# A fixed order on TensorE for the attention part of a decoder trunk: scores in runs of 14 or 16, transposes from the third projection step on, value products of two units in a row

## The chip, the cores and the metric

The kernel runs on one core of a Trainium2 chip. The metric is the device time of one execution in microseconds (us); it is given as the median of several executions. The profile is of one execution, whose own time is given beside it.

## The reference, cut to what matters

One gated short-convolution layer is followed by one layer of dilated sliding-window attention, each with a feed-forward block behind it. There are 512 tokens, 1024 features, 16 heads of 64 and three branches, whose softmaxes are joined by their log-sum-exp. The part that matters here is the attention:

```python
s = jnp.einsum("brhnqd,brhnkd->brhnqk", qb, kk).astype(jnp.float32)
...
s = jnp.where(mask, s, NEG_INF)
m = jnp.max(s, axis=-1)
p = jnp.exp(s - m[..., None])
l = jnp.sum(p, axis=-1)
o = jnp.einsum("brhnqk,brhnkd->brhnqd", p, vv.astype(jnp.float32)) / l[..., None]
lse = m + jnp.log(l)
...
wts = jax.nn.softmax(jnp.stack(lses, axis=0), axis=0)
o = jnp.einsum("gbsh,gbshd->bshd", wts, jnp.stack(outs, axis=0))
return o.astype(x.dtype).reshape(B, S, N_HEADS * HEAD_DIM) @ w_o
```

## The kernel before, in words

All projections split their operands into a high and a low part and run three products. A weight block of 128x8x256 comes in by one DMA as `raw`; VectorE multiplies it by a gain (L113), ScalarE casts the high part `wh` (L93) and VectorE subtracts it to get `wl` (L94). There are buffers for three such blocks (six `wh`, six `wl`) and two for `raw`.

The attention goes over four groups of four heads (`for i in range(NG)`, L757). A group has six projection steps (`rope_mms`, q and k of three branches): each is 48 matmuls of 512 columns into two banks of the tag "mm" (`feature_mm`, L140), and then `rope` (L527): eight ScalarE copies into `sw`, then six VectorE operations. Behind the steps come three value projections (`values`, L645), each in two pieces of 48 matmuls of 256 columns (L658).

Between these the small matmuls of the attention are placed:

- Scores (`scores`, L577): q and k of one head are 64 rows high, and the two heads of a pair stand on rows 0 to 63 and 64 to 127; an output is 128x128 in a bank of the tag "at". VectorE adds the mask, writes `p` and takes the maximum in one operation (L597), ScalarE takes the exponent (L607). There are two parts, two head pairs and four blocks of queries, so 60 score matmuls in a group. The profile shows each as two passes.
- `factors` (L610) exchanges the row sums of the two parts by small DMAs and makes the joint softmax factors.
- `transposed` (L676): VectorE scales `p` by the factor (L685), TensorE transposes it (L688, 60 in a group) into two "at" banks for a unit, ScalarE copies each bank to a tile `trs` (L690). These tiles come from the same four buffers as `sw`.
- `times_v` (L693): value products with 64 output rows (L717, 60 in a group, two passes each) into a bank `o`, which ScalarE copies out.

A unit is one head pair, one part and two of the four blocks, so there are eight in a group. `fill` (L753) runs two entries of a list behind each piece and each step: scores behind the pieces of the value projections, units behind the steps of the next group. Each tag, "mm" and "at", has four PSUM banks. In the last group the first steps of the output projection (`wo_step`, L513) stand where the next group's steps would be, and `heads_x` (L745) writes its operands `xh`, `xl` into the memory that the value projections read.

The code is recorded, and a scheduler then orders the instructions of each engine, unless `tc.issue_after` ties one behind another. It also picks the buffer that a new tile takes. So before the change, where a score matmul or a value product stands among the projections is the scheduler's choice, save for this:

```python
with tc.issue_after(mark) if mark else nullcontext():
    m = nc.tensor.matmul(
        out, v, rhs, start=first, stop=part == 0 and e == 1,
        skip_group_check=True).ins
if first:
    mark = m
```

Of the kernel before, what the change touches and what calls it, by code (L numbers as in the profile page):

```python
# [15 lines left out]
P = 128  # L16
T = 512
NT = T // P
D = 1024
KT = D // P  # L20
# [6 lines left out]
NG = 4  # L27
# [11 lines left out]
def trunk(  # L39
# [82 lines left out]
    def feature_mm(jobs, t0, t1, attn):  # L122
# [15 lines left out]
        for i, (k, p) in enumerate(todo):  # L138
            for ps, (_, (wh, wl)) in zip(outs, jobs):
                nc.tensor.matmul(ps, (wh, wl, wh)[p][:, k, :], x[p == 2][:, k],  # L140
                                 start=i == 0, stop=i == len(todo) - 1)
# [9 lines left out]
    def feature_mms(makers, between=None, attn=False, marks=((),) * 4):  # L151
# [5 lines left out]
        if between is None:  # L157
            pairs = [m() for m in makers]
            for i in range(0, len(pairs), 2):
                feature_mm(pairs[i:i + 2], 0, NT, attn)  # L160
            return [ps for ps, _ in pairs]
# [18 lines left out]
    def token_mm(outs, ah, al, wh, wl, first, last):  # L180

        for i, o in enumerate(outs):
            nc.tensor.matmul(o, ah, wh[i], start=first, stop=False)  # L183
# [329 lines left out]
    def wo_step(k, tt, n):  # L513
        wh, wl = ws[4 * n + k // 2]
        return token_mm([ys[tt][n]], xh[:, tt, k, :], xl[:, tt, k, :],
                        [wh[:, k % 2, :]], [wl[:, k % 2, :]], k == 0, k == KT - 1)

    with ExitStack() as inner:
# [24 lines left out]
        def rope_mms(g, i, rest, fill):  # L543
# [4 lines left out]
            for src, gain in ((w_q[0], gq), (w_kv, gkv)):  # L548
                tag = "at" if ms and rest else "mm"
                ms += makers(tag, load_cols(src, c0), gain)  # L550
                if not rest:
                    d += [rope(ps, f"qk{g}", g) for ps in feature_mms(ms[-2:], None, True)]
# [9 lines left out]
        class Heads:  # L562
# [14 lines left out]
            def scores(self, part, pr, b2):  # L577

                st = self.st[part]
                ps = [bank("at", "s").rearrange("p (b k) -> p b k", b=2) for _ in range(2)]  # L580
                for b in (b2, b2 + 1):
                    for e in range(2):
# [4 lines left out]
                        for h2 in range(2):  # L587
                            rw = slice(64 * h2, 64 * h2 + 64)
                            nc.tensor.matmul(  # L589
                                ps[h2][:, b - b2, e * P:(e + 1) * P],  # L590
                                q[pr][rw, b * P:(b + 1) * P], k[pr][rw, kb * P:(kb + 1) * P],
                                start=True, stop=True)
                    lo = 128 if part == 0 and b == 0 else 0
                    mask = (maskA, maskB)[part]
                    for h2 in range(2):
                        hh = 2 * pr + h2
                        nc.vector.tensor_tensor_reduce(  # L597
                            self.p(part, hh, b), ps[h2][:, b - b2, lo:], mask[:, lo:],
                            1.0, -3.0e38, ALU.add, ALU.max, st[:, b, hh, 0:1])
                if b2 == 0:  # L600
                    return
# [43 lines left out]
            def values(self, g):  # L645
# [7 lines left out]
                def piece(n):  # L653
                    for k in range(KT):
                        wh, wl = (x[:, k % 4, :] for x in w[k // 4])
                        for p in range(3):
                            for m in range(2):
                                nc.tensor.matmul(  # L658
                                    ps[m][:, n, :], (zh, zh, zl)[p][:, k, 2 * m + n],
                                    (wh, wl, wh)[p],  # L660
                                    start=k == 0 and p == 0, stop=k == KT - 1 and p == 2)
# [14 lines left out]
            def transposed(self, pr, part, hh, b2):  # L676
# [5 lines left out]
                for b in (b2, b2 + 1):  # L682
# [4 lines left out]
                    for e in range(lo, 256, P):  # L687
                        nc.tensor.transpose(  # L688
                            tr[:, b - b2, e:e + P], p[:, e - lo:e - lo + P], ident)
# [3 lines left out]
            def times_v(self, pr, part, b2, trs):  # L693
# [5 lines left out]
                mark = None  # L699
                for b in (b2, b2 + 1):  # L700
                    for e in range(2):
                        if part == 0 and b + e == 0:
                            continue
                        for hh in range(2):
# [11 lines left out]
                            with tc.issue_after(mark) if mark else nullcontext():  # L716
                                m = nc.tensor.matmul(  # L717
                                    out, v, rhs, start=first, stop=part == 0 and e == 1,
                                    skip_group_check=True).ins
                            if first:  # L720
                                mark = m
# [8 lines left out]
            def units(self):  # L730

                def unit(pr, part, b2):
                    self.flight.append(((pr, part, b2), [
                        self.transposed(pr, part, hh, b2) for hh in (2 * pr, 2 * pr + 1)]))
                    if len(self.flight) > 1:
                        self.rest()

                return [lambda a=(pr, part, b2): unit(*a)
# [125 lines left out]
```

## Time and profile before

| what | before |
|---|---|
| median of 3 runs | 1498.02 us |
| lowest and highest | 1497.49 and 1499.73 us |
| the profiled execution: its time | 1498.81 us |
| its span | 1497.0 us |
| granted TensorE clock, mean | 0.999 |
| PE busy | 1484.5 us (99%) |
| PEld, DVE, ACT busy | 1256.2, 741.6, 615.6 us |

The span is the time from the first to the last instruction of the program; the execution's time lies 1.8 us above it. PE is TensorE's matmuls, PEld its weight loads, DVE VectorE, ACT ScalarE. Matmuls overlap, so that an instruction's own duration is longer than the time until the next one can start.

### The profile page before, as it was taken

Reading aid. Unit: us, or ns where it says so; the run is one execution under the profiler, and the core shown is the slowest. Engines: PE = TensorE matmul, PEld = TensorE weight load, DVE = VectorE, ACT = ScalarE, POOL = GpSimd, SP = SyncE. Lnnn points to the kernel's source line nnn. Section 1 sums busy time; section 2 is a strip of 40 time slices with the busy share of each in tenths; the row PEclk is TensorE's granted clock in tenths of the full one; section 3 lists DMA queues with packets and bytes.
Section 4 is the critical chain, followed back from the end, with each engine's and each line's share of the span. In section 5 each row is a group of like instructions: output and inputs, shape, how many; then the busy total and the mean of one; then the engine's idle time right before and its main releaser. Section 6 shows DMA issues by size and latency. Waiting matters only on the chain.

```text
span 1497.0 us, 19969 instructions
## 1 busy us (share of the span) xinstructions
PE 1484.5 (99%) x8155; PEld 1256.2 (84%) x8155; DVE 741.6 (50%) x1312; ACT 615.6 (41%) x1133; POOL 58.2 (4%) x108
## 2 busy tenths in 40 slices
PE   9999999999999999999999999999999999999998
PEld 8888898888888889898788889889879888888886
DVE  5735453323233368767667566765546332323332
ACT  5313342212123236574666557466554221212321
POOL 1000100000000020000001001000010000000000
PEclk9999999999999999999999999999999999999999
DMA  6343033223323303222122212212123322332311
GB/s 219 107 141 109 33 113 113 72 98 113 123 88 113 113 29 113 85 86 86 57 65 79 85 64 81 85 57 86 31 85 113 113 71 98 113 124 87 113 57 56
DMA packets 110369, 137.43 MB, mean 92 GB/s; under 512 B 3485, under 2 KB 99013, under 8 KB 110278
## 3 DMA queue, kind: packets, MB, share of 16 engines
q1 hardware_dynamic: 108708, 135.56, 27.2%
q8 instruction: 64, 1.05, 0.3%
q0 software_dynamic: 1280, 0.26, 0.2%
q10 hardware_dynamic: 290, 0.33, 0.1%
q14 instruction: 27, 0.22, 0.0%
HBM read 133.92 MB, written 2.23 MB: 91 GB/s over the span
## 4 chain that ended last, share of the span: by engine, by line
PE 66%; issue 26%; DMA 3%; DVE 2%; POOL 1%; ACT 1%; POOLq 0%; DVEq 0%; SPq 0%; ACTq 0%
PE mmf L140 26%; PE atf L140 14%; PE vps L658 8%; PE s L589 2%; PE o L717 2%; PE tr L688 2%; DMA raw<-in_w_kv 1%; DVE raw L113 1%; DMA raw<-in_ffn_w_gate_up 1%; POOL y L207 1%; DMA raw<-in_w_q 1%; DVE wl L94 1%; POOL a L205 1%; PE y1b L187 0%; PE y1a L183 0%
## 5 line engine op out<-in xcount | busy, mean ns | idle before, releaser
L94 DVE TENSOR_TENSOR wl<-raw,wh 128x1024 fp32r<-128x1024 f32 x244 | 292.9, 1222 | 74.6 <-ACT wh L93 74.2
L93 ACT CAST wh<-raw 128x1024 fp32r<-128x1024 f32 x244 | 246.8, 1047 | 104.3 <-PE atf L140 42.7
L140 PE MATMUL mmf<-xh,wh 128*128 128x512 f32 (+1 forms) x848 | 275.2, 377 | 2.8 <-ACT xh L93 2.8
L140 PE MATMUL mmf<-xl,wh 128*128 128x512 f32 (+1 forms) x848 | 271.4, 374 | 0.0
L140 PE MATMUL mmf<-xh,wl 128*128 128x512 f32 (+1 forms) x848 | 270.7, 374 | 0.0
L140 PE MATMUL atf<-xh,wh 128*128 128x512 f32 (+1 forms) x560 | 181.0, 365 | 0.0
L140 PE MATMUL atf<-xl,wh 128*128 128x512 f32 (+1 forms) x560 | 180.1, 365 | 0.0
L140 PE MATMUL atf<-xh,wl 128*128 128x512 f32 (+1 forms) x560 | 180.0, 365 | 0.0
L140 PEld LDWEIGHTS mmf<-xh,wh 128*128 128x128 f32 x848 | 152.8, 188 | 32.5 <-ACT xh L93 3.5
L366 DVE TENSOR_TENSOR act<-atf,s 128x512 f32<-128x512 f32 x44 | 30.4, 692 | 301.6 <-ACT s L365 301.6
L140 PEld LDWEIGHTS mmf<-xl,wh 128*128 128x128 f32 x848 | 153.3, 188 | 28.7 <-issue 0.9
L140 PEld LDWEIGHTS mmf<-xh,wl 128*128 128x128 f32 x848 | 153.3, 188 | 27.9
L365 ACT ACTIVATE s<-mmf 128x512 f32<-128x512 f32 x44 | 26.3, 598 | 334.9 <-PE mmf L140 326.7
L113 DVE TENSOR_TENSOR raw<-raw,cols 128x512 f32<-128x512 f32 x144 | 90.4, 686 | 85.7 <-DMA raw<-in_w_kv 60.5
L140 PEld LDWEIGHTS atf<-xl,wh 128*128 128x128 f32 x560 | 99.5, 189 | 16.9
L140 PEld LDWEIGHTS atf<-xh,wl 128*128 128x128 f32 x560 | 99.5, 189 | 17.0
L140 PEld LDWEIGHTS atf<-xh,wh 128*128 128x128 f32 x560 | 99.6, 188 | 16.6
L536 ACT COPY sw<-mmf 32x512 f32<-32x512 f32 x92 | 53.3, 579 | 78.7 <-PE mmf L140 71.4
L658 PE MATMUL vps<-wh,xh 128*128 128x256 f32 x384 | 81.2, 289 | 0.0
L658 PE MATMUL vps<-wh,xl 128*128 128x256 f32 x384 | 79.3, 286 | 0.0
L658 PE MATMUL vps<-wl,xh 128*128 128x256 f32 x384 | 79.1, 285 | 0.0
L94 DVE TENSOR_TENSOR al<-act,ah 128x512 fp32r<-128x512 f32 x44 | 30.2, 691 | 96.4 <-ACT ah L93 96.4
(182 smaller groups left out, 1993.6 us busy)
## 6 DMA issues: line engine op xcount, KB each, us to landing
raw<-in_ffn_w_gate_up SPq DMA_DIRECT2D x44, 1024.0 KB, 6.6
raw<-in_w_kv SPq DMA_DIRECT2D x24, 1024.0 KB, 5.2
raw<-in_ffn_w_down SPq DMA_DIRECT2D x22, 1024.0 KB, 4.8
raw<-in_w_q SPq DMA_DIRECT2D x12, 1024.0 KB, 5.2
raw<-in_conv_w_in SPq DMA_DIRECT2D x11, 1024.0 KB, 5.1
raw<-in_conv_w_out SPq DMA_DIRECT2D x4, 1024.0 KB, 4.8
raw<-in_w_o SPq DMA_DIRECT2D x4, 1024.0 KB, 5.0
h<-in_x SPq DMA_DIRECT2D x4, 512.0 KB, 7.1
```

What stands on the lines that cost most here:

```text
L93: return [nc.scalar.copy(hi, src).ins, nc.vector.tensor_tensor(lo, src, hi.bitcast(F32), ALU.subtract).ins]
L94: nc.vector.tensor_tensor(lo, src, hi.bitcast(F32), ALU.subtract).ins]
L113: nc.vector.tensor_tensor(src[:, ks], src[:, ks], g.broadcast_to([P, a // 2, b]), ALU.mult)
L140: nc.tensor.matmul(ps, (wh, wl, wh)[p][:, k, :], x[p == 2][:, k], start=i == 0, stop=i == len(todo) - 1)
L205: nc.gpsimd.tensor_scalar(a, ssq[:, 0:1], EPS, ssq[:, 1:2], ALU.add, ALU.add)
L365: nc.scalar.activation(s, ps[2 * j], AF.Silu)
L366: nc.vector.tensor_tensor(act[2 * c + j], ps[2 * j + 1], s, ALU.mult)
L536: nc.scalar.copy(w[s:s + 32], y[s + 32:s + 64])
L589: nc.tensor.matmul(ps[h2][:, b - b2, e * P:(e + 1) * P], q[pr][rw, b * P:(b + 1) * P], k[pr][rw, kb * P:(kb + 1) * P], start=True, stop=True)
L658: nc.tensor.matmul(ps[m][:, n, :], (zh, zh, zl)[p][:, k, 2 * m + n], (wh, wl, wh)[p], start=k == 0 and p == 0, stop=k == KT - 1 and p == 2)
L688: nc.tensor.transpose(tr[:, b - b2, e:e + P], p[:, e - lo:e - lo + P], ident)
L717: m = nc.tensor.matmul(out, v, rhs, start=first, stop=part == 0 and e == 1, skip_group_check=True).ins
```

## The change

A helper `strict` ties each matmul that goes through it behind the one before it, so that these keep the order of the code. The projection steps (when they get a `fill`), the value projections, scores, transposes, value products and the first output steps all go through it. A call of `scores` now does all four blocks of a head pair: 14 or 16 score matmuls into four "at" banks, then the eight mask operations. `fill` runs one entry, in the middle of a step and behind it, and ahead of each value piece. Three empty entries put the first unit behind the second step. A unit is transposed alone, and every second call first runs the value products of the two units before it.

```diff
+    traced = []
+    def strict(op, *args, **kwargs):
+        with tc.issue_after(traced[0]) if traced else nullcontext():
+            traced[:] = [op(*args, **kwargs).ins]
...
         for i, (k, p) in enumerate(todo):
+            if fill and i == len(todo) // 2:
+                fill()
             for ps, (_, (wh, wl)) in zip(outs, jobs):
...
+                if fill:
+                    strict(nc.tensor.matmul, *args, **kwargs)
...
-            def scores(self, part, pr, b2):
+            def scores(self, part, pr):
 
                 st = self.st[part]
-                ps = [bank("at", "s").rearrange("p (b k) -> p b k", b=2) for _ in range(2)]
-                for b in (b2, b2 + 1):
+                banks = [[bank("at", "s").rearrange("p (b k) -> p b k", b=2) for _ in range(2)]
+                         for _ in range(2)]
+                for b in range(NT):
...
                         for h2 in range(2):
                             rw = slice(64 * h2, 64 * h2 + 64)
-                            nc.tensor.matmul(
-                                ps[h2][:, b - b2, e * P:(e + 1) * P],
-                                q[pr][rw, b * P:(b + 1) * P], k[pr][rw, kb * P:(kb + 1) * P],
-                                start=True, stop=True)
+                            strict(nc.tensor.matmul,
+                                   banks[b // 2][h2][:, b % 2, e * P:(e + 1) * P],
+                                   q[pr][rw, b * P:(b + 1) * P], k[pr][rw, kb * P:(kb + 1) * P],
+                                   start=True, stop=True)
+                for b in range(NT):
                     lo = 128 if part == 0 and b == 0 else 0
...
-                def unit(pr, part, b2):
-                    self.flight.append(((pr, part, b2), [
-                        self.transposed(pr, part, hh, b2) for hh in (2 * pr, 2 * pr + 1)]))
-                    if len(self.flight) > 1:
+                def unit(n, what):
+                    if n % 2 == 0:
                         self.rest()
...
+                    if what:
+                        pr, part, b2 = what
+                        self.flight.append((what, [
+                            self.transposed(pr, part, hh, b2) for hh in (2 * pr, 2 * pr + 1)]))
...
             def rest(self):
-                what, trs = self.flight.pop(0)
-                self.times_v(*what, trs)
+                for what, trs in self.flight:
+                    self.times_v(*what, trs)
+                self.flight.clear()
...
         def fill():
-            for f in todo[:2]:
-                f()
-            del todo[:2]
+            if todo:
+                todo.pop(0)()
...
                 for piece in heads.values(g):
+                    fill()
                     piece()
-                    fill()
             heads.factors()
-            todo = heads.units()
+
+            todo += [lambda: None] * (3 if i < NG - 1 else 0) + heads.units()
```

What the change moves is shown at three places; a row is a line of the code, an operation, output and inputs, and the output's size, and behind "waits" the engines or DMA queues whose semaphores it waits for.

TensorE in the value projections of the second group, before: the score matmuls (`s`) of the second head pair stand singly and by fours among the projection's matmuls (`vps`).

```order
L589 MATMUL s<-qk_5361,qk_5234 128x128
L658 MATMUL vps<-wh,xh 128x256 x2
L658 MATMUL vps<-wl,xh 128x256 x2
L658 MATMUL vps<-wh,xl 128x256 x2
L658 MATMUL vps<-wh,xh 128x256 x2
L658 MATMUL vps<-wl,xh 128x256
L589 MATMUL s<-qk_5361,qk_5234 128x128
L658 MATMUL vps<-wl,xh 128x256
L658 MATMUL vps<-wh,xl 128x256 x2
L658 MATMUL vps<-wh,xh 128x256
L589 MATMUL s<-qk_5361,qk_5234 128x128 x4
```

TensorE at the start of the same value projections, in the changed kernel: the last value products (`o`) of the first group, then all 14 score matmuls of the first head pair, then the first projection's matmuls (all of them come through the helper, L127).

```order
L127 MATMUL o<-trs,v_4618 64x4x32 [waits Activation_49] x2
L127 MATMUL o<-trs,v_4618 64x4x32 x6
L127 MATMUL s<-qk_5307,qk_5225 128x128 [waits PE_49] x2
L127 MATMUL s<-qk_5307,qk_5225 128x128 x4
L127 MATMUL s<-qk_5307,qk_5225 128x128 [waits PE_49]
L127 MATMUL s<-qk_5307,qk_5225 128x128 [waits DVE_49,PE_49]
L127 MATMUL s<-qk_5307,qk_5225 128x128 x6
L127 MATMUL vps<-wh,xh 128x256 x2
```

Value products and scores now follow each other in one piece, 14 instructions each, and the eighth score matmul, the first into the fourth bank, waits for VectorE.

VectorE at that place, in the changed kernel: the gains of a coming block, the low part of the third value projection's weights, and then the first mask operations of these scores (`p,st<-s`).

```order
L113 TENSOR_TENSOR raw<-raw,cols 128x4x128 x3
L94 TENSOR_TENSOR wl<-raw,wh 128x1024 [waits Activation_49] x2
L619 ISA p_5857,st_5859<-s,cst 128x128 [waits DMASW3_49,DMASW2_49,PE_49]
L619 ISA st_5859 128x1
L619 ISA p_5857,st_5859<-s,cst 128x256
```

The mask operations that free the first bank stand behind two weight splits; the program's semaphores say that the eighth score matmul waits for the second mask operation, since its tile takes the bank of the unit's first tile.

VectorE in the last group, in the changed kernel: the end of `factors`, three low parts of the output projection's operand (`xl`), and the scalings of `p` that the transposes wait for.

```order
L661 RECIPROCAL f_8921<-f_8921 128x16 [waits DVE_49]
L94 TENSOR_TENSOR xl<-O,xh 128x4x128 [waits PE_49,Activation_49]
L662 TENSOR_TENSOR f_8907<-f_8907,ea 128x16 [waits DVE_49]
L662 TENSOR_TENSOR f_8921<-f_8921,ea 128x16 [waits DVE_49]
L94 TENSOR_TENSOR xl<-O,xh 128x4x128 [waits PE_49,Activation_49]
L705 TENSOR_SCALAR p_8371<-p_8371,f_8907 128x128 [waits DVE_49]
L94 TENSOR_TENSOR xl<-O,xh 128x4x128 [waits PE_49,Activation_49]
L705 TENSOR_SCALAR p_8372<-p_8372,f_8921 128x256 [waits DVE_49]
```

Before, all six of these low parts stood ahead of `factors`; now three stand between its last operations and the first scaling that a transpose needs, and each waits for the last matmuls of the value projection.

## Rows read from the trace of the kernel before

**Rows 1.** The page: TensorE's busy time, share of the span, instructions.

```profile
PE 1484.5 (99%) x8155; PEld 1256.2 (84%) x8155; DVE 741.6 (50%) x1312; ACT 615.6 (41%) x1133; POOL 58.2 (4%) x108
```

**Rows 2.** Four stretches, by group: length, busy us (instructions) by engine, clock, DMA.

```profile
624.89:756.49 131.60, 131.38 (x877) 111.72 (x876) 89.65 (x213) 80.21 (x173) 6.12 (x10) 1.00 0.25 78
756.49:885.88 129.39, 129.39 (x878) 110.93 (x877) 87.01 (x210) 79.54 (x172) 5.88 (x10) 1.00 0.24 76
885.88:1015.34 129.46, 129.46 (x878) 110.96 (x877) 87.06 (x210) 79.56 (x172) 5.87 (x10) 1.00 0.24 74
1015.34:1099.15 83.81, 83.14 (x673) 72.91 (x671) 40.02 (x140) 50.44 (x127) 5.87 (x10) 1.00 0.14 48
```

**Rows 3.** Timeline of PE, third group: start us, us, engine, line, operation.

```profile
884.06 0.61 PE L140 MATMUL mmf<-xl,wh 128*128 128x512 f32 x2
...
885.88 0.40 PE L658 MATMUL vps<-wh,xh 128*128 128x256 f32 x2
...
891.39 0.40 PE L658 MATMUL vps<-wh,xl 128*128 128x256 f32 x2
891.72 0.94 PE L589 MATMUL s<-qk,qk 64*128 64x128 f32 x12
892.59 0.50 PE L658 MATMUL vps<-wh,xh 128*128 128x256 f32 x2
892.93 0.39 PE L658 MATMUL vps<-wl,xh 128*128 128x256 f32 x2
```

**Rows 4.** Timeline of PE, a score run of 16 passes in the last group.

```profile
1040.07 0.40 PE L658 MATMUL vps<-wh,xl 128*128 128x256 f32 x2
1040.40 1.16 PE L589 MATMUL s<-qk,qk 64*128 64x128 f32 x16
...
1041.83 0.40 PE L658 MATMUL vps<-wl,xh 128*128 128x256 f32 x2
```

**Rows 5.** Timeline of PE, a run of value products between transposes.

```profile
707.04 0.87 PE L688 MATMUL tr<-ident,p 128*128 128x128 f32 x6
707.84 1.09 PE L717 MATMUL o<-trs,v 128*64 128x128 f32 x16
708.87 0.66 PE L688 MATMUL tr<-ident,p 128*128 128x128 f32 x4
709.28 0.48 PE L140 MATMUL mmf<-xh,wh 128*128 128x512 f32 x1
```

**Rows 6.** Timeline of ACT at the end of a group's steps.

```profile
885.90 0.58 ACT L536 COPY sw<-mmf 32x512 f32<-32x512 f32 x1 [5.38 <-PE mmf L140]
...
890.65 1.99 ACT L93 CAST wh<-raw 128x1024 fp32r<-128x1024 f32 x2
```

**Rows 7.** Timeline of DVE behind a run of scores.

```profile
1044.58 0.42 DVE L597 CUSTOM_DVE_ANT_0 p<-s,cst 128x256 f32<-128x256 f32 x1 [1.91 <-PE s L589]
...
1044.93 0.42 DVE L597 CUSTOM_DVE_ANT_0 p<-s,cst 128x256 f32<-128x256 f32 x1
```

**Rows 8.** Timeline of all engines, last group, from its last projections to its transposes.

```profile
1060.24 6.28 DVE L94 TENSOR_TENSOR xl<-O,xh 128x512 fp32r<-128x512 f32 x6 [5.00 <-ACT xh L93]
...
1062.82 0.40 PE L183 MATMUL y<-wh,xh 128*128 128x512 f32 x1
...
1068.21 8.22 DVE L685 TENSOR_SCALAR p<-p,f 128x128 f32<-128x128 f32 x32
...
1074.41 1.91 PE L688 MATMUL tr<-ident,p 128*128 128x128 f32 x16
1075.04 2.06 ACT L690 COPY trs<-tr 128x512 f32<-128x512 f32 x4 [7.66 <-PE tr L688]
```

**Rows 9.** Timeline of all engines, the end of the last group.

```profile
1096.59 1.89 PE L717 MATMUL o<-trs,v 128*64 128x128 f32 x28
...
1099.15 0.50 PE L183 MATMUL y<-wh,xh 128*128 128x512 f32 x1 [0.68 <-ACT xh L93]
...
1100.08 3.50 DVE L94 TENSOR_TENSOR wl<-raw,wh 128x1024 fp32r<-128x1024 f32 x3 [0.26 <-ACT wh L93]
```

More of the change, by code (lines that the diff above doesn't have):

```diff
@@ L178, in makers, with token_mm @@
                 for j in range(2)]
-    def token_mm(outs, ah, al, wh, wl, first, last):
+    def token_mm(outs, ah, al, wh, wl, first, last, strictly=False):
+        if strictly:
+            for i, o in enumerate(outs):
+                strict(nc.tensor.matmul, o, ah, wh[i], start=first, stop=False)
+                strict(nc.tensor.matmul, o, ah, wl[i], start=False, stop=False)
+                strict(nc.tensor.matmul, o, al, wh[i], start=False, stop=last)
+            return
         for i, o in enumerate(outs):
@@ L551, in rope_mms @@
                 if not rest:
-                    d += [rope(ps, f"qk{g}", g) for ps in feature_mms(ms[-2:], None, True)]
+                    d += [rope(ps, f"qk{g}", g) for ps in feature_mms(
+                        ms[-2:], None, True, fill=fill)]
                     fill()
@@ L597, in scores @@
                         nc.vector.tensor_tensor_reduce(
-                            self.p(part, hh, b), ps[h2][:, b - b2, lo:], mask[:, lo:],
+                            self.p(part, hh, b), banks[b // 2][h2][:, b % 2, lo:], mask[:, lo:],
                             1.0, -3.0e38, ALU.add, ALU.max, st[:, b, hh, 0:1])
-                if b2 == 0:
-                    return
                 for hh in (2 * pr, 2 * pr + 1):
@@ L657, in piece @@
                             for m in range(2):
[L658 to L661, printed above, removed]
+                                strict(nc.tensor.matmul,
+                                       ps[m][:, n, :], (zh, zh, zl)[p][:, k, 2 * m + n],
+                                       (wh, wl, wh)[p],
+                                       start=k == 0 and p == 0, stop=k == KT - 1 and p == 2)
                     if n:
@@ L715, in times_v @@
                             first = new and b == 0 and e == 0
[L716 to L721, printed above, removed]
+                            strict(nc.tensor.matmul, out, v, rhs, start=first,
+                                   stop=part == 0 and e == 1, skip_group_check=True)
                 if part == 1 or b2 == 0:
@@ L760, in trunk @@
                   for g in range(NB)]
[L761 to L762 removed]
+            while todo:
+                fill()
             if pp is None:
@@ L766, in trunk @@
             heads = Heads(i, qk)
-            todo = [lambda a=(part, pr, b2): heads.scores(*a)
-                    for part in range(2) for pr in range(2) for b2 in (0, 2)]
+            todo += [lambda a=(part, pr): heads.scores(*a)
+                     for part in range(2) for pr in range(2)]
             for g in range(NB):
                 for piece in heads.values(g):
+                    fill()
                     piece()
-                    fill()
             heads.factors()
-            todo = heads.units()
+            todo += [lambda: None] * (3 if i < NG - 1 else 0) + heads.units()
         load_wo(0)
```

33 lines of the change are left out of this document (16 added, 17 removed).

## The prediction

> **What bounds the kernel now.** I read the busy times first: TensorE (PE) works for 99% of the span, and no other engine reaches 51% [rows 1]. Then the four groups of the attention, each from the end of one group's projection steps to the end of the next group's, the last to its last value product [rows 2]: PE is busy for 131.38 of 131.60 us, 129.39 of 129.39, 129.46 of 129.46, and 83.14 of 83.81, with the clock at 1.00. So there is no wait here that the change could take away. It can only make PE's own work shorter, or add waits. The next question is what PE's time is made of, and for that I read the distances between starts, since matmuls overlap. From 884.06 eight matmuls of 512 columns start in 1.82 us until the projection of values begins at 885.88: 0.2275 each. From there 46 of 256 columns take 5.51 us to 891.39: 0.12 each [rows 3]. A group has 288 of either kind, 65.5 and 34.5 us, and 60 transposes of 0.11, 6.5 us. What is left of a group, scores and value products, is 131.6 − 106.5 = 25.1 us in the first, 22.9 and 23.0 in the next two. The last has 84 matmuls of 512 columns (19.1 us), so 83.8 − 19.1 − 34.5 − 6.5 = 23.7, of which 0.7 are a wait at its end that has nothing to do with the change [rows 9], so 23.0. I forecast **faster**, since this remainder is more than the same products cost in longer runs.
>
> **What a run of scores costs.** A run is a row of small matmuls with nothing else between them. In one of 12 passes, from 891.39 to 892.93 are 1.54 us with four matmuls of 0.12, which leaves 1.06 for the run [rows 3]. In one of 16, from 1040.07 to 1041.83 are 1.76, which leaves 1.28 [rows 4]. The difference of four passes is 0.22, or 0.055 a pass, and 1.06 − 12×0.055 = 0.40 is the price of entering and leaving a run, paid whatever its length. For value products the only row between transposes has 16 passes: from 707.04 to 708.87 are 1.83 us less six transposes, 1.18, so 0.30 and 16×0.055 [rows 5]. That they too cost 0.055 a pass is my choice. The upper bound is the 28 passes of 1.89 us against 16 of 1.09 [rows 5, 9], 0.067 a pass, with a smaller fixed price then.
>
> **What the change removes.** A group has 60 score matmuls and 60 value products, 120 passes each. At 0.055 they are 13.2 us, so about 9.8 of the 23 are prices of entering and leaving; runs of 12 [rows 3] are among the longer ones, others have one or four matmuls, as the order shows. The changed kernel has four runs of scores in a group (28, 28, 32, 32 passes) and four of value products (32, 28, 32, 28). By the prices above these are 2×1.94 + 2×2.16 + 2×2.06 + 2×1.84 = 16.0 us. The saving is 9.1 + 6.9 + 7.0 + 7.0 = 30.0 over the four groups. In the last group the scheduler still parts one run of value products in three, between matmuls of the output projection: two more runs, −0.8. That makes 29.2. At 0.067 a pass for value products (0.10 fixed), their two longer forms cost 2.24 and 1.98, together 0.6 more in a group: 26.6 instead of 29.2.
>
> **What the change adds: the wait for the fourth bank.** In groups 2 to 4 the first run of scores follows at once upon the last run of value products. Its eighth matmul waits until VectorE has read the first tile. From the end of the steps VectorE has two low parts ahead of that, which wait for ScalarE's two casts of 1.0 each [rows 6]. With 0.2 for the first to start, the first low part can begin at about 1.3. The two take 1.17 each [rows 9], to 3.6, and the two mask operations begin 0.35 apart and last 0.42 [rows 7], to 4.35. PE arrives after the value products (1.84) and seven score matmuls (14 passes and half a fixed price, 0.97): 2.8. It then waits 1.5 us, three times: 4.5. Behind this matmul stand seven more and all of the value projection, so nothing covers it. If VectorE placed the masks ahead of the low parts, it would be nothing; the order says that it doesn't.
>
> **What the change adds: the last group.** The first transposes wait for `p` scaled, and VectorE has three low parts `xl` ahead. Six of them take 6.28 now [rows 8], so 1.03 apart. They wait for the value projection's last matmul, since they overwrite what it reads. So a transpose can start about 0.3 + 3×1.03 + 0.2 + 2×0.26 (32 scalings in 8.22 [rows 8]) = 4.2 us behind that matmul; PE has only nine matmuls of the output projection first, 2.05 us. A wait of about 2.2 us, 2.3 with the pipeline. Before, PE did not meet it: its first transpose in these rows comes at 1074.41, 6.2 us after the scalings begin at 1068.21 [rows 8]. Both waits together cost 6.8.
>
> **What I cost at nothing.** The eight mask operations behind a run take 8×0.35 = 2.8 us and hold all four "at" banks [rows 7]; the 48 value-projection matmuls behind each run take 5.76 and cover them [rows 3]. Without that cover each of 16 runs would wait 0.7. Masks and casts themselves do not change in number. The transposes move to where two runs of 24 matmuls of 512 columns (10.9 us) and eight transposes lie between a unit's transposes and its value products, 11.8 in all. ScalarE has two casts (2.0) and eight rope copies (885.90 to 890.65, 4.75 [rows 6]) at a step's end, 6.7 us, and then a unit's two copies, 4 for 2.06 [rows 8], so they are done near 7.8. That leaves 4 us. No DMA is issued at another place in its queue that PE waits for: the traffic in the groups is 0.14 to 0.25 of the engines [rows 2].
>
> The Trainium skill, TensorEngine Tiling (Array Packing), section PSUM Bottleneck, speaks against the change: tiles of the array speed up TensorE but not the emptying of PSUM, and the copies may become the bottleneck. By that rule a run of scores in four banks would be paced by its 2.8 us of mask operations. The cover above, 5.76 us, says no, and the sum goes by the cover; the third rival below prices the other way.
>
> **The sum.** 29.2 − 6.8 = 22.4. The profiled execution took 1498.8, so 1476.4; the median is 0.8 lower, and the same saving from it gives 1475.6. I forecast **1476**. With the other price a pass it is 1478.6. A measurement of this kernel tells about 0.2%, 3 us, from no change.
>
> **The rivals.**
> *No new waits.* VectorE's and ScalarE's queues may run ahead of PE so far that the low parts are done before PE arrives. For it: PE has not once waited in three of the groups. Against it: the casts and the `xl` both need the end of PE's own work just before. It gives 1498 − 29.2 = 1469.
> *Reading the scores paces them.* If the low parts and gains that stand among the masks delay these beyond the cover, each of 16 runs waits about the 0.7 above (2.8 − 2.06), 11.9 us in all. For it: VectorE is busy for 87 of 129 us in a group. Against it: 5.76 of cover. It gives 1476 + 11.9, about 1488.
> *Slower: value products wait for their copies.* The copies to `trs` stand behind casts and rope copies on ScalarE and share four buffers with the latter. If they came 4 us later than worked out, PE would begin to wait at each of the 16 runs, and from 1.4 us of wait a run (22.4/16) the change loses. At 2 us it gives 1498 − 22.4 + 32 = 1508. For it: ScalarE has nine casts or copies ahead of the first of them. Against it: it is idle for 50 of 129 us in a group.
> *The change doesn't do what it says.* If the fixed price were not one of a run but of each pass or of the first product in a bank, longer runs would save nothing, and the waits remain: 1498 + 6.8 = 1505. Against it: 12 and 16 passes differ by 0.055 a pass, far below 1.06/12.
>
> **How the numbers follow.** The forecast has 0.62, with a range of its own of 1472 (half of the waits) to 1481 (the higher price a pass, 2.6, and 2 us of waits more). No new waits has 0.12, pacing by the masks 0.13, the slower rival 0.06, a price that isn't saved 0.03, and 0.04 is left for savings and waits that cancel. The range goes from 1467, a little below the second case, to 1488, and leaves out about 0.15. Faster than 1495 are the first three and no other: 0.87; within 3 us 0.04, slower 0.09.
>
> **What would show it.** Runs of 28 and 32 passes in 1.9 to 2.2 us; groups 2 and 3 (from one end of the steps to the next) of 106.5 + 16.0 + 1.5 = 124.0 us where 129.4 stand; an idle time of PE of 1.5 us ahead of the eighth score matmul in three groups, released by VectorE; one of 2.2 ahead of the last group's first transpose, released by a scaling of `p`; ScalarE's copies of `trs` done 4 us ahead of their products; the clock still at 1.00. The forecast is wrong if a longer run costs over 0.067 a pass, if PE idles over 5 us elsewhere in the groups, or if time is lost outside them, which the change doesn't touch.

## The result

The changed kernel takes 1482.28 us (median of 4, 1480.96 to 1483.45), the kernel before 1498.01 (1497.49 to 1499.73). The ratio is 0.9892, 95% interval 0.9879 to 0.9904: 15.7 us faster. The forecast was 1476; the time lies in its wide range (1467 to 1488), and just above the likeliest case's own range of 1472 to 1481. The profiled execution took 1480.96 with a span of 1479.1, so in the trace the saving is 17.9 where 22.4 were forecast. The points below go by the trace.

### The profile after

By the page (as [rows 1]) TensorE is busy for 1461.5 us, still 99%, of a span that is 17.9 shorter.

The four stretches of the attention, cut as in [rows 2] (at the end of each group's steps and value products):

```profile
624.73:749.23 124.50, 123.54 (x878) 108.53 (x877) 91.54 (x218) 81.25 (x174) 6.13 (x10) 1.00 0.27 86
749.23:873.40 124.17, 122.98 (x879) 108.43 (x877) 86.90 (x211) 79.10 (x173) 5.88 (x10) 1.00 0.24 78
873.40:998.33 124.93, 123.56 (x879) 108.80 (x877) 84.40 (x207) 78.92 (x173) 5.87 (x10) 1.00 0.24 77
998.33:1080.04 81.71, 78.38 (x675) 69.99 (x673) 38.41 (x140) 49.08 (x127) 5.87 (x10) 1.00 0.17 53
```

Against 131.60, 129.39, 129.46 and 83.81 they are 7.1, 5.2, 4.5 and 2.1 us shorter, 18.9 in all. PE is no longer busy for the whole of a stretch: 1.0, 1.2, 1.4 and 3.3 us of each are idle. The view of waits names what ended the idle time (total, times, longest):

```profile
PE s L127 <- DVE st L619: 3.6, 3, 1.2
PE mmf L154 <- ACT xh L93: 2.2, 3, 1.3
...
PE y L127 <- ACT v L686: 1.2, 1, 1.2
PE o L127 <- ACT trs L710: 1.1, 2, 1.0
...
PE tr L127 <- DVE p L705: 0.2, 1, 0.2
```

**The runs.** In PE's timeline a run of 28 score passes stands between two value projections; one starts 1.77 us before the next matmul:

```profile
632.11 0.40 PE L127 MATMUL vps<-wh,xl 128*128 128x256 f32 x2
632.44 1.83 PE L127 MATMUL s<-qk,qk 64*128 64x128 f32 x28
634.21 0.50 PE L127 MATMUL vps<-wh,xh 128*128 128x256 f32 x2
634.55 0.39 PE L127 MATMUL vps<-wl,xh 128*128 128x256 f32 x2
```

From 632.11 to 634.55 are 2.44, less four matmuls of 0.12: 1.96, where 1.94 was worked out. A run of 32 passes, read in the same way at 640.14, costs 2.17 where 2.16 was worked out.

**The wait for the fourth bank.** The first run of the second group, in PE's timeline, right behind the value products, and VectorE's at the same time:

```profile
747.55 1.75 PE L127 MATMUL o<-trs,v 128*64 128x128 f32 x28
749.23 1.16 PE L127 MATMUL s<-qk,qk 64*128 64x128 f32 x14
751.57 1.13 PE L127 MATMUL s<-qk,qk 64*128 64x128 f32 x14 [1.19 <-DVE st L619]
752.62 0.50 PE L127 MATMUL vps<-wh,xh 128*128 128x256 f32 x2
```
```profile
748.51 2.36 DVE L94 TENSOR_TENSOR wl<-raw,wh 128x1024 fp32r<-128x1024 f32 x2 [4.42 <-ACT wh L93]
750.78 0.28 DVE L619 CUSTOM_DVE_ANT_0 p<-s,cst 128x128 f32<-128x128 f32 x1
750.99 0.42 DVE L619 CUSTOM_DVE_ANT_0 p<-s,cst 128x256 f32<-128x256 f32 x1
```

Seven matmuls (14 passes), then the stop; the second mask operation ends at 751.41, and the eighth matmul starts at 751.57, 4.0 behind the steps' end (4.35 was worked out). The run takes 3.39 instead of 1.77: 1.62 lost, three times.

**The copies that I had given 4 us of slack.** ScalarE's and VectorE's timelines ahead of the first group's first value products, which start at 702.19 and stall in the middle; behind them, from all three engines, the lines at the second run of products, which starts at 717.11:

```profile
695.95 1.57 ACT L710 COPY trs<-tr 128x512 f32<-128x512 f32 x3
702.81 0.59 ACT L710 COPY trs<-tr 128x512 f32<-128x512 f32 x1 [5.28 <-DVE qk L559]
```
```profile
698.46 2.50 DVE L113 TENSOR_TENSOR raw<-raw,cols 128x512 f32<-128x512 f32 x4 [0.91 <-DMA raw<-in_w_kv]
700.88 1.22 DVE L94 TENSOR_TENSOR wl<-raw,wh 128x1024 fp32r<-128x1024 f32 x1
702.01 0.69 DVE L559 TENSOR_TENSOR qk<-qk,sw 128x512 f32<-128x512 f32 x1
```
```profile
717.72 0.69 DVE L559 TENSOR_TENSOR qk<-qk,sw 128x512 f32<-128x512 f32 x1
718.51 0.58 ACT L710 COPY trs<-tr 128x512 f32<-128x512 f32 x1 [2.42 <-DVE qk L559]
719.15 1.09 PE L127 MATMUL o<-trs,v 128*64 128x128 f32 x14 [0.96 <-ACT trs L710]
```

Three copies are early, near 697. The fourth needs one of the four buffers, which the rope's last operation frees; that stands on VectorE behind four gains (2.50 us, begun 0.91 late for a weight block's DMA) and a low part (1.22). In the second run of products the stop is longer: there two sets of gains stand ahead of the rope's last operation, and the first waits 3.16 for its DMA. From the start of a run to the next matmul the two runs take 2.27 and 3.06 us; the same two in the second group's products, where the same copies come just in time, take 1.90 and 1.68.

**The last group.** The view books the idle time in another place than forecast: the seventh matmul of the output projection waits for a bank that ScalarE copies out behind three casts of `xh`, and the transposes then hardly wait.

```profile
1044.81 1.07 ACT L686 COPY v<-vps 128x512 f32<-128x512 f32 x2
...
1045.25 1.07 DVE L94 TENSOR_TENSOR xl<-O,xh 128x512 fp32r<-128x512 f32 x1
1045.44 0.50 PE L127 MATMUL y<-wh,xh 128*128 128x512 f32 x1 [1.24 <-ACT v L686]
...
1046.23 2.90 DVE L705 TENSOR_SCALAR p<-p,f 128x256 f32<-128x256 f32 x11
1046.63 1.22 PE L127 MATMUL tr<-ident,p 128*128 128x128 f32 x8 [0.23 <-DVE p L705]
```

The bank hides the forecast wait and does not replace it. The scaling that releases the first transpose stands behind the third `xl`, as forecast, and starts at 1046.23, so the transpose starts at 1046.63, 3.98 behind the value projection's end (1042.65), where 4.2 was worked out. By these lines PE, with the bank free at once, would have stood at the transpose instead; no run shows that alone.

**The clock.** It is not at 1.00 throughout. Behind the end of the attention, after PE's two short waits (0.7 and 0.5) for ScalarE and VectorE there, a window reads as below (third figure from the end: eight matmuls in 3.30 us at 0.50, the 1.2 GHz level); from 1086.00 to 1088.00 the clock is 1.00 again:

```profile
1082.30:1085.60 3.30, 3.30 (x8) 2.62 (x9) 3.30 (x4) 2.06 (x4) 0.00 (x0) 0.50 0.29 71
```

### The profile page after: what moved, and what is told of

It reads as the page before. It is cut to its first block, busy times and chain, and to the rows that moved or that the text cites. A ratio compares the mean times of both kernels' runs of the same rounds, so it can differ in the third digit from the quotient of the medians.

```text
span 1479.1 us, 20013 instructions
## 1 busy us (share of the span) xinstructions
PE 1461.5 (99%) x8155; PEld 1247.2 (84%) x8155; DVE 739.9 (50%) x1312; ACT 614.2 (42%) x1133; POOL 57.8 (4%) x108
## 4 chain that ended last, share of the span: by engine, by line
PE 64%; issue 27%; DVE 4%; DMA 3%; POOL 1%; ACT 1%; POOLq 0%; DVEq 0%; SPq 0%; ACTq 0%
PE atf L154 14%; PE mmf L127 12%; PE mmf L154 11%; PE vps L127 9%; PE s L127 2%; PE tr L127 1%; DMA raw<-in_w_kv 1%; PE o L127 1%; DVE wl L94 1%; DVE raw L113 1%; PE y L127 1%; POOL y L226 1%; DVE p L705 1%; PE y L204 1%; POOL a L224 1%
## 5 line engine op out<-in xcount | busy, mean ns | idle before, releaser
L154 PE MATMUL mmf<-xh,wh 128*128 128x512 f32 (+1 forms) x496 | 161.7, 363 | 2.2 <-ACT xh L93 2.2
L154 PE MATMUL mmf<-xl,wh 128*128 128x512 f32 (+1 forms) x496 | 160.6, 362 | 0.0
L154 PE MATMUL mmf<-xh,wl 128*128 128x512 f32 (+1 forms) x496 | 160.4, 362 | 0.0
L127 PE MATMUL mmf<-xh,wh 128*128 128x512 f32 x352 | 111.0, 396 | 0.0
L127 PE MATMUL mmf<-xh,wl 128*128 128x512 f32 x352 | 108.8, 390 | 0.0
L127 PE MATMUL mmf<-xl,wh 128*128 128x512 f32 x352 | 108.6, 390 | 0.0
L154 PEld LDWEIGHTS mmf<-xh,wh 128*128 128x128 f32 x496 | 87.8, 189 | 17.4 <-ACT xh L93 2.9
L154 PEld LDWEIGHTS mmf<-xl,wh 128*128 128x128 f32 x496 | 87.5, 189 | 14.2
L154 PEld LDWEIGHTS mmf<-xh,wl 128*128 128x128 f32 x496 | 87.5, 189 | 14.3
L127 PE MATMUL vps<-wh,xh 128*128 128x256 f32 x384 | 79.0, 288 | 0.0
```

The costliest lines, as they stand in the source:

```text
L127: traced[:] = [op(*args, **kwargs).ins]
L154: nc.tensor.matmul(*args, **kwargs)
```

## The experiments

The diffs are against the changed kernel, unless the text says otherwise. Each has 4 to 11 executions against 9 to 15 of the kernel before on the same chip (medians 1498.1 to 1499.0). A trace is of one execution, and this one can lie off the median: it took 2.4 us more in the first run below, 1.5 in the second, 3.1 in the products' part alone and 3.2 in the gains behind the rope, and 1.3 less in the changed kernel, 2.1 in the last group's operands later and 2.9 in one unit in a row.

### The scores one piece later

```diff
                 for piece in heads.values(g):
-                    fill()
                     piece()
+                    fill()
```

> The changed kernel, with each run of scores behind a piece of the value projection instead of ahead of it; the runs and their lengths stay. Theory (the wait of the eighth score matmul in groups 2 to 4 comes from VectorE's two low parts at the end of the steps): the three idle times of 1.46 us ahead of it go, the run pays 0.2 us more for entering, so 4.3 us less than the 1482.3 of the changed kernel, about 1478. Rival (reading the scores is slow wherever the run stands, the masks pace it): the wait only moves, and the time stays within 2 us of 1482.

Measured: 1483.11 (1481.96 to 1485.49), ratio 0.9893 (0.9878 to 0.9909). The time is the rival's, the reason is neither's. The scores no longer wait. The waits of PE are others:

```profile
PE tr L127 <- DVE p L705: 2.4, 1, 2.4
PE y L127 <- ACT v L686: 2.0, 1, 2.0
PE mmf L127 <- DVE qk L557: 1.8, 3, 0.8
PE o L127 <- ACT trs L710: 1.5, 3, 0.9
```

The scores end a piece later, so exponents, factors and scalings do too. In the last group the first transpose follows after nine matmuls; that stretch, from the end of its value projections, is the last row of the windows of this kernel, and here that of the changed kernel with those of the three periods before it (from one end of the value projections to the next):

```profile
1042.82:1085.71 42.89, 37.89 (x266) 30.14 (x264) 14.70 (x55) 14.08 (x28) 1.84 (x4) 0.92 0.07 25
```
```profile
667.43:793.55 126.12, 123.97 (x878) 108.80 (x877) 87.70 (x211) 79.03 (x172) 7.03 (x13) 1.00 0.25 78
793.55:917.73 124.18, 123.00 (x878) 108.45 (x877) 86.36 (x210) 78.98 (x172) 5.03 (x10) 1.00 0.24 77
917.73:1042.65 124.92, 123.55 (x878) 108.79 (x877) 83.70 (x215) 82.36 (x179) 6.83 (x12) 1.00 0.26 86
1042.65:1080.04 37.39, 35.25 (x267) 27.90 (x265) 12.05 (x39) 12.76 (x24) 0.00 (x0) 1.00 0.08 29
```

42.89 against 37.39: 5.5 given back in this trace. Nearly half of it is the lower clock (0.92 on the mean): behind the wait eight transposes and nine output matmuls take 1.62 and 3.99 us, in the changed kernel 0.98 and 2.16.

### Runs of scores cut in two

```diff
+                        if k == KT // 2:
+                            fill()
...
-            def scores(self, part, pr):
+            def scores(self, part, pr, b2):
```

on top of the kernel of the run before, with two banks instead of four.

> As the run before this one, but each run of scores is cut in two (12 or 16 passes), with 24 matmuls of the value projection between the halves: 32 runs instead of 16, with the same passes. Theory (a fixed price of 0.40 us for entering and leaving a run): 16 x 0.40 = 6.4 us more than the uncut form, about 1484.5. Rival (the price is one of each pass, or of a wait that longer runs avoid): within 1.5 us of the uncut form.

Measured: 1484.42 (1484.17 to 1485.87), ratio 0.9902 (0.9888 to 0.9916), 1.3 more than uncut, not 6.4: by the time alone the rival's case. Yet the price is there. PE's timeline has the two halves:

```profile
753.85 0.40 PE L127 MATMUL vps<-wh,xl 128*128 128x256 f32 x2
754.18 0.94 PE L127 MATMUL s<-qk,qk 64*128 64x128 f32 x12
...
755.39 0.39 PE L127 MATMUL vps<-wl,xh 128*128 128x256 f32 x2
```

The first half costs 755.39 − 753.85 − 0.48 = 1.06, the second (16 passes, at 758.10) 1.28 as in [rows 4], together 2.34, against 1.96 for 28 passes in one run: 0.38 for one run more. Sixteen of them are 6.1. Added up from start to start, scores and value projection take 1.55 us more in each of the three periods than uncut, which is four runs at 0.39. They are bought back: steps, transposes and value products take 6.9 less in the three periods. This kernel's value products and projection steps have no wait at all in the attention, where the uncut form's have 1.5 and 1.8 in the rows above; the rest of the 6.9 shows in no row of the waits.

### The scores' part alone

The kernel before, with `scores`, `values` and `strict` of the change and one run ahead of each piece.

> The kernel before, with the scores' part of the change alone (14 or 16 score matmuls in a run ahead of each piece); transposes and value products are placed as before the change. 51 runs of scores become 16: their price in the trace of before is 53.5 us in all, and 16 runs of 28 or 32 passes cost 32.8, so 20.7 less. Theory: the wait of the eighth score matmul is longer here, since no value products stand between the end of the steps and the scores: 4.1 us behind the steps' end against 0.97, so 3.1 us in three groups, 9.4; 1498 - 20.7 + 9.4 = about 1487. Rival (no such wait, or masks ahead of the low parts here): about 1477.5.

Measured: 1486.1 (1484.61 to 1489.71), ratio 0.9914 (0.9898 to 0.9929). Near the theory's time, but by another way: the scores wait for nothing. At the same place, without value products ahead, all 28 passes run through (PE's timeline), because the last value products come earlier here and ScalarE has copied their bank out long before (its timeline). No mask can have freed a bank for them: VectorE's first one here starts at 754.68, when the run is over.

```profile
750.25 1.83 PE L127 MATMUL s<-qk,qk 64*128 64x128 f32 x28
```
```profile
744.22 0.59 ACT L733 COPY O<-o 128x512 f32<-128x512 f32 x1
```

So what is short in the changed kernel is a bank: `o` holds one of four until ScalarE copies it. Part of what the scores save is lost again to transposes that wait for copies and scalings (1.7 and 1.1 us in this kernel's waits) and to 41 runs of value products instead of 38. That is under 4 of some 8 us that are missing from the 20.7; the rest was not followed.

### The products' part alone

```diff
-                    fill()
                     piece()
+                    fill()
+                    fill()
```

with `scores` and `values` of before.

> The changed kernel, with the scores and the value projection in the order of before (runs of 2 to 8 score matmuls, by the scheduler); transposes and value products as in the change. 38 runs of value products (41.0 us in the trace of before) become 18 (31.8): 9.2 less. Theory: the waits that the changed kernel has for the copies of transposes (2.5), in the last group (1.8) and the lower clock behind its end (1.6) stay here, since they hang on the products' order: 1498 - 9.2 + 5.9 = about 1494.5. Rival (those waits come from the scores' runs, which delay VectorE): about 1489.

Measured: 1501.01 (1499.91 to 1504.11), ratio 1.0013 (1.0004 to 1.0022): no gain, where the theory had 1494.5 and the rival 1489. Both are missed. Its waits:

```profile
PE mmf L154 <- ACT xh L93: 4.1, 2, 3.0
PE tr L127 <- DVE p L705: 2.4, 1, 2.4
```

The scores end late here as in the first experiment, and the transposes of the last group have only nine matmuls ahead of them: the stretch from the end of its value projections takes 42.19, against 36.33 cut likewise in the kernel before, 5.9 more.

```profile
1062.25:1104.44 42.19, 37.71 (x266) 29.99 (x264) 14.18 (x54) 13.55 (x28) 1.29 (x3) 0.92 0.08 25
```

The first wait is far outside, near 206 us, where no edit reaches: 3.0 here against 1.3 in the changed kernel. It differs from trace to trace, and may be one reason why executions of one kernel spread by some us. The clock there is 0.79 over 8.1 us, against 1.00 in the changed kernel.

The products' gain itself is in the trace. Added up from start to start, steps, transposes and value products take 2.2 us less than in the kernel before in each of the second and the third period, for five runs of value products fewer. But scores and value projection, in the scheduler's order again, take 1.5 more in the second. The three periods are 131.17, 128.70 and 126.50, 2.8 less in all than before.

### Gains behind the rope

```diff
+                with behind(turned[-5:][:1]):
                     nc.vector.tensor_tensor(
                         src[:, ks], src[:, ks], g.broadcast_to([P, a // 2, b]), ALU.mult)
...
+            turned.append(m.ins)
             return dst
```

> The changed kernel, with one order more on VectorE: the gains of a block that comes three steps later stand behind the last operation of the rope, which frees the buffer that a transpose's copy needs. Theory (the value products' waits of 0.4 to 1.4 us in two groups come from a copy that waits for that operation, which stands behind gains that wait for a weight block's DMA): 2.5 us less than the changed kernel, about 1480. Rival (the copies are late because ScalarE is, whatever VectorE does): the waits stay, within 1 us of 1482.3.

Measured: 1489.82 (1489.26 to 1493.03), ratio 0.9936 (0.9923 to 0.995). The waits for the copies are gone, and the three periods are now all the same, 124.18, 124.17 and 124.17 (the first in the windows, cut as above):

```profile
683.49:807.67 124.18, 122.99 (x878) 108.40 (x877) 88.51 (x211) 79.18 (x172) 5.67 (x10) 1.00 0.24 78
```

That is 2.7 less than 126.12 + 124.18 + 124.92, where the theory said 2.5. Run by run, 2.5 of the 2.7 lie in the two runs of products above and the same two of the third period. But the first blocks have no rope three steps ahead, so that my edit put them behind the first rope there is, and PE waits for their weights in the first group's steps; from 589 to 603 us the clock is 0.60. The first period starts 16.1 later than in the changed kernel:

```profile
PE mmf L128 <- ACT wh L93: 5.9, 2, 5.8
...
PE mmf L128 <- DVE wl L94: 3.2, 2, 2.8
```

### The same, later

The list `turned` is filled only from the second group's steps on.

> As the run with the gains behind the rope, but not in the first group's steps, where PE waited 9 us for the weights that this made late. Theory: groups 2 to 4 keep their 124.2 us from one end of the value projections to the next, 2.7 less than the changed kernel's three, and the first steps come back: about 1479.6. Rival (the lower clock and the waits vary by as much from one execution to the next): within 1.5 us of 1482.3.

Measured: 1492.52 (1491.99 to 1496.55), ratio 0.9967 (0.9956 to 0.9978). The same slip one group later: the first period takes 138.04 (clock 0.95), the other two 124.18 and 124.16. The theory's 1479.6 and the rival's 1482.3 are both missed. The cause of the waits for the copies is shown by these two runs; a version that only gains was not had.

### The last group's operands later

```diff
-        for k in range(6):
+        for k in range(3):
             heads_x(k, O[:, k, :])
...
             f()
+            if n == 1:
+                with behind(copies + scaled[-1:]):
+                    for k in range(3, 6):
+                        heads_x(k, O[:, k, :])
```

> The changed kernel, with three of the six operands of the output projection split later in the last group: behind ScalarE's copies of the last value projection and behind VectorE's first scalings. Theory: the wait of 1.24 us of the seventh output matmul (for a bank that ScalarE copies out behind three casts) and the 0.23 us of the first transpose go: 1.5 to 1.8 us less, about 1480.6. Rival (the transposes then wait for the scalings behind the factors, as the prediction had it): 0.5 us less or nothing.

Measured: 1479.34 (1477.29 to 1480.27), ratio 0.9864 (0.985 to 0.9877): the fastest kernel here, about 3 us below the changed one. Both waits are gone (its last stretch of the attention, windows):

```profile
1041.77:1077.53 35.76, 34.95 (x267) 27.95 (x265) 13.16 (x40) 13.68 (x25) 0.00 (x0) 1.00 0.08 30
```

35.76 against 37.39 is 1.6. In the traces 3.7 are gained: 1.2 more lie behind the attention, where the clock stays at 1.00 in this profile, and 0.8 in the periods ahead, which the edit doesn't touch. The edit brings the copies of `v` and the scalings forward together, so it doesn't part the two waits.

### One unit in a row

```diff
-                    if n % 2 == 0:
+                    if n > 1:
                         self.rest()
```

with one unit taken in `rest`.

> The changed kernel, with the value products of one unit in a row, each two entries behind its transposes, instead of two units: 29 runs instead of 18, with the same passes. Theory (a fixed price of 0.30 us a run): 11 x 0.30 = 3.3 us more, about 1485.6, if the waits for the copies stay as they are. Rival (products in twos cost waits for copies that single ones do not): 1482 or less.

Measured: 1484.69 (1481.84 to 1485.46), ratio 0.9898 (0.9885 to 0.9912), 2.4 more than the changed kernel. The intervals overlap, so the time alone doesn't decide. Its value products wait for nothing (1.1 us in the changed kernel's waits), so 3.3 − 1.1 = 2.2 would be the theory's. The second period decides, which in the changed kernel (124.18) has no wait for a copy (windows):

```profile
793.52:918.84 125.32, 124.10 (x879) 108.09 (x878) 85.96 (x210) 78.98 (x172) 4.57 (x9) 1.00 0.24 76
```

It has seven runs of value products instead of four and is 1.14 longer. A stop of a transpose near 836.8 is 0.2 of that; the rest is 0.3 a run, as the theory has it.

### The three together, and the first run in mid-piece

> The three changes in one: scores behind the pieces, gains behind the rope, the last group's operands split later. If the waits are independent: 4.3 + 2.5 + 1.7 = 8.5 us less than the changed kernel, about 1473.8. Rival (a wait that is taken away comes back at another place, since VectorE and ScalarE have the same work to do in the same time): 1477 or more.

Measured: 1492.62 (1491.8 to 1492.99), ratio 0.9954 (0.9941 to 0.9966). It holds the slip of the gains, and a wait of 4.3 us of the last group's first transpose for its scaling. Between them, with the scores behind their pieces and the copies in time, the three periods take 123.28, 123.10 and 123.34 (the second in the windows), the shortest of all and 0.8 to 1.1 under the 124.17 of the gains behind the rope:

```profile
804.45:927.55 123.10, 122.93 (x879) 108.14 (x877) 87.60 (x210) 78.81 (x173) 5.89 (x10) 1.00 0.25 78
```

So the later scores do gain there; the stretch behind the last period takes 42.15, against 37.39 in the changed kernel, and gives that back.

The next kernel puts only the first run of groups 2 to 4 into the middle of the first piece:

```diff
-                    fill()
+                    if not mid:
+                        fill()
                     piece()
...
+                        if k == KT // 2 and mid:
+                            fill()
```

> The changed kernel, with only the first run of scores of groups 2 to 4 moved: into the middle of the first piece of the value projection; the later runs stay, so that the last scores of a group are no later. Theory (putting all runs one piece later, the first run of this list, won 1.46 us three times at the scores but made the factors late by a piece, and VectorE's scalings and the transposes behind them waited instead): here the three waits go and none comes, 4.9 - 0.1 = 4.8 us less than the changed kernel's own 1482.3, 1477.5. Rival (the scores' wait only ever moves, since VectorE is behind at the end of the steps): 1481 or more.

Measured: 1482.94 (1482.49 to 1483.51), ratio 0.9896 (0.9883 to 0.991). The rival's time. The eighth matmul waits a little longer than before (1.37 against 1.19), now for another bank and another engine (PE's timeline, and the copy in ScalarE's):

```profile
754.98 1.16 PE L127 MATMUL s<-qk,qk 64*128 64x128 f32 x14 [1.37 <-ACT O L743]
```
```profile
754.34 0.58 ACT L743 COPY O<-o 128x512 f32<-128x512 f32 x1
```

The copy of `o` stands behind two casts and eight rope copies, so its bank is free only near 754.9. That fits the scores' part alone (copied early: no wait) and the first experiment (a whole piece ahead, 5.9 us: no wait). In groups 2 and 3 the second run of scores, now only half a piece behind the first, stops too: it takes 3.01 instead of 1.76 (759.12 to 762.13), released by mask operations, which share VectorE with rope operations and four gains. Here reading the scores does pace a run, as the prediction's rival had it. Copying `o` ahead of the rope was not tried.

> The last group's operands split later (1479.3 by itself) and the first run of scores in mid-piece. If the two are independent: 4.8 less than 1479.3, 1474.5. Rival (the value products' waits for the copies grow when the steps come sooner, as they did with all runs one piece later): 1477 or more.

Measured: 1481.4 (1481.28 to 1483.58), ratio 0.9889 (0.9876 to 0.9903): 2.1 more than the last group's change alone, so nothing is gained on top of it.

> As the run before, with the gains behind the rope as well, not in the first group's steps. Theory: the three periods of 123.2 us of the version with scores one piece later, the changed kernel's last group less 1.6 and no start lost: 1472.5. Rival (with the scores in mid-piece VectorE's order costs another wait): not below 1474.5.

Measured: 1493.92 (1493.41 to 1495.13), ratio 0.9971 (0.9959 to 0.9983): the slip of the gains again.

## Why the prediction was right, and where it was not

The direction and the main term, the price of a run, came out as worked out. The likeliest case's own range ended at 1481 and was missed by 1.3 us, for the reasons below; the measured time lies in the part of the range that was left for a rival.

**The price of a run: right.** 0.055 a pass and 0.40 a run gave 1.94 for 28 passes, measured 1.96; the cut runs give 0.38 for one more. For value products 0.055 a pass was a choice, and it holds: two runs without a wait, of 32 and 28 passes, take 1.90 and 1.68 to the next matmul (828.11 and 842.65), 0.055 a pass and not 0.067; one unit in a row gives 0.3 for one run more. In the second group 124.17 − 106.5 − 1.62 of waiting leaves 16.05, where 16.0 was forecast. The Trainium skill, TensorEngine Tiling (Array Packing), section Key Properties, says that changing the tiling mode drains TensorE. It states no price. The traces fit it, with 0.4 us a run of scores; that a drain is what costs it, no run shows.

**The wait for the fourth bank: right in place and size, too narrow in cause.** 1.5 forecast, 1.62 measured, three times 4.9. VectorE's low parts end it, as forecast; but it exists because `o` holds a bank. Three runs show it: no wait where `o` is copied early, the same wait for `o` itself in mid-piece, none a whole piece later.

**The last group: right, with another wait ahead of it.** The first transpose started 3.98 behind the value projection's end, 4.2 forecast. Nine matmuls ahead of it take 2.1, so 1.9 are lost where 2.2 were worked out; 1.6 come back in the run without them. That the view books 1.24 of it on the bank of `y`, behind ScalarE's casts, the prediction did not foresee. The two runs of value products that the scheduler parts off in this group are priced there at 0.4 each, where its own price for them is 0.3; that is 0.2 in the sum.

**"That leaves 4 us" for the copies of the transposes: wrong.** This is the step that failed, in a forecast that came out right as a whole. I counted ScalarE's work and took the shared buffers as free. The fourth copy waits for VectorE's last rope operation, which stands behind gains that wait for a DMA. It cost 2.7 us in the first and third group (what goes with the gains behind the rope), and is the slower rival's wait in a small form: in some of the runs of products, not in all 16.

**The clock: not foreseen.** The prediction had it at 1.00, and named time lost outside the groups as a sign of being wrong. The stretch behind the attention is 1.2 us longer (397.85 to the end of the span before, 399.06 now), with 3.3 us at half clock in it.

So by the stretches I had forecast 9.1, 5.4, 5.5 and 2.4 us; 7.1, 5.2, 4.5 and 2.1 came. That is 3.5 less, and with the 1.2 behind the attention 4.7, where 22.4 − 17.9 = 4.5 are missing. The other 2 us, between the traces and the medians, are the two profiled executions' places in their spread; of the changed kernel's other executions there is no trace, so what makes them longer is open.

The rule of the Trainium skill that I had weighed (TensorEngine Tiling (Array Packing), section PSUM Bottleneck: tiles don't empty PSUM faster) did not pace the runs of the changed kernel, which have a whole piece between them: apart from the first run of groups 2 to 4, none waits. With half a piece between them one does (the run in mid-piece); the rival that the prediction means by this rule, and calls the third, is its second. The rule was right in kind: most of the waits that the change brought are for a bank or a buffer that ScalarE or VectorE has still to empty; the first transpose's is for a scaling.

## What to carry to other kernels

Small matmuls that use half of TensorE's rows or columns should stand in long runs: here one run less gains 0.3 us (value products) to 0.4 us (scores), whatever its length. When PE is 99% busy, a fixed order turns slack into waits: list each bank and buffer that a run needs, who frees it, and what stands ahead of that on its engine, its DMAs too. Moving the waiting instruction later gained nothing in all here, since the work that follows from it (exponents, factors, scalings) came later as well and cost more in the last group than the periods had gained, or the wait went to the next bank; the scores behind their pieces in all groups but the last was not tried. When one wait is gone, ask what the next one on the list would end: the last group had two that ended within 1.2 us of each other. Taking other work from ahead of the releasing instruction did help.

## What had not been expected of the hardware

PE's clock fell to 0.50 for 3.3 us behind two waits of 0.7 and 0.5 us, while in the run with the last group's operands later, and in the kernel before, the same two waits are followed by full clock. In the traces of four other kernels (the scores one piece later, the runs cut in two, the products alone, the three together) it fell in the last group (0.92 over some 42 us) behind waits of 1.2 to 4.3. Which waits are followed by a drop is not settled by these runs.
